# A two-block network in one program: five PSUM banks for dense products, zeros multiplied first, more context products behind the norms

## The chip, the cores and the metric

One Trainium2 chip, one core. The metric is the device time of one launch in microseconds, the median of repeated runs. Everything is computed in fp32 or in pairs of fp32r values (a rounded high part and the rest).

## What is computed

The reference chains two transformer blocks on a sequence of 256 tokens with a model width of 1024. The first block is a normalised mixer of three attentions with gates, then a convolutional feed-forward. The second block, run twice (layer 0 and layer 1), mixes a differential attention and a state-space scan (SSD) for two streams, the 256 latent tokens `x` and 256 context tokens `ctx`, each normalised and modulated by its own conditioning, and ends with a squared-ReLU MLP. Cut to what the change touches:

```
def modulate(x, g, shift, scale):
    return rmsnorm(x, g) * (1 + scale) + shift

for l in range(2):
    h_l = modulate(xl, norm_mix_g[l], mod_l[0], mod_l[1])
    h_c = modulate(xc, norm_mix_g[l], mod_c[0], mod_c[1])
    o_l, o_c = hybrid_mixer_2(h_l, h_c, ...)          # q, k, v, z, conv inputs, gates = h @ w_in
    xl = xl + mod_l[2] * o_l
    xl = xl + mod_l[5] * sq_relu_mlp(modulate(xl, norm_mlp_g[l], mod_l[3], mod_l[4]), w_mlp1[l], w_mlp2[l])
    ...                                               # the same for xc in layer 0
```

## The kernel before, in words

Activations lie transposed, features on the 128 partitions, eight tiles of 128 features each; `h` is such a set of eight (high, low) pairs, with columns 0 to 255 for the latent tokens and 256 to 511 for the context. A weight piece is 128 x 1024 values: SyncE loads it (`wr`), ScalarE rounds it (`wh`, L207), VectorE subtracts to get the rest (`wl`, L208). A dense product with one piece is 24 matmuls: for each of eight k-tiles high by high, high by low and low by high (L225 to L227 with the weight held in the array, L246 to L248 with the activation held).

The order on TensorE is written out: each stage is a Python generator of dense work (one or two steps for each product), and `weave` (L185) lets every generator in a list `bg` of background work go one step after each step of dense work. On the other engines the order comes from priorities. A background generator's `yield` therefore says how many dense steps lie between two of its pieces on TensorE. `wait` in `norm` (L284) adds such steps.

A norm (L284) squares the eight tiles on ScalarE (L296), adds them on VectorE (L298), sums over partitions with small matmuls (L307), takes the power on GpSimd (L269), makes diagonals on VectorE (L273, `dg`) and spreads them with a matmul (L281). `mod_norm` (L926) then makes for each tile `u` on VectorE (L939), `v` from it on GpSimd (L940), the high part on ScalarE (L941) and the low part on VectorE (L942). `u` and `v` come from `tmp()`; in the second block these are the pool `mt` with six buffers.

The places that the change touches, in order of time:

- the start of `first_block`: the products `prods_c` run on unnormalised activations while `pre_norm` computes the norm;
- the post-norm of the first block (`add_normed`, L871), behind which four products of the context's gates are woven (`gate_blocks`, pieces 72 to 75);
- the chain behind the feed-forward: `add_normed`, two empty steps, `mod_norm` for the second block (L859 to L863), behind which `ssd_lead` (L1078) computes `S.nv` value products of the context ahead of time, two dense steps each, stores them in `vd`, and `diff_front` (L1301) later loads them and leaves out the context half of that head pair's value product;
- in `layer`, the dense products behind the attention's last head pair: `diff_front` of head pair 3 and `gate_blocks` with pieces 80 to 87 (512 columns each in layer 0, in two steps);
- in `layer` 0, `mod_norm` of the MLP, woven into the first MLP products (`up`, L1628), whose results wait in PSUM for `r` (L1635) on ScalarE.

PSUM has eight banks: three for `mm` (dense products), three for `sm`, two for `lg` (used only by the SSD and by the attention).

Of the kernel before, what the change touches and what calls it, by code (L numbers as in the profile page):

```python
# [10 lines left out]
F32 = mybir.dt.float32  # L11
# [6 lines left out]
P = 128  # L18
# [80 lines left out]
class Net:  # L99
    def __init__(self, ctx, tc, A, stop=None, x_only=False):  # L100
# [11 lines left out]
        self.ps_lg = p("pslg", 2, space=PSUM)  # L112
        self.sp = p("sp", 2)
        self.HP = 100
        self.MW = 2
# [12 lines left out]
        nc = self.nc  # L128
# [5 lines left out]
        warm = self.cp.tile([P, 4], F32, name="warm")  # L134
        nc.scalar.activation(warm, self.nhalf, AF.Copy)

    def constants(self, first):
# [28 lines left out]

    def mm_ps(self, shape=(P, 512)):
        return self.ps_mm.tile(list(shape), F32, tag="mm", name="mm")

# [166 lines left out]
    def first_block(self, es_x):  # L336
# [5 lines left out]
        with ExitStack() as es:  # L342
# [46 lines left out]
            bc = []  # L389
# [3 lines left out]
            def pre_norm():  # L393
                t1 = lambda: p4.tile([P, 256], F32, tag="t1", name="hv")
                sq = []
                for c in range(4):
                    t = pb.tile([P, 2, 256], F32, tag=f"gate{c}", name="sq")
                    sq += [t[:, 0, :], t[:, 1, :]]
                yield from self.norm(x, lambda: sq.pop(), bc, start=True)
                nc.scalar.activation(rt, bc[0], AF.Copy)  # L400
                nc.vector.tensor_copy(rc, bc[1][:, 0:2])
                yield
                for k in range(8):
                    v = t1()
                    nc.vector.scalar_tensor_tensor(v, x[k], self.sm("pre_g", k), rt, op0=ALU.mult, op1=ALU.mult)
                    self.split(h[k][0], h[k][1], v)
# [343 lines left out]
            hcd = tc.dram_tile([8, P, 2, 256], F32, name="hcd")  # L750
            gd = self.gd = tc.dram_tile([8, P, 512], F32, name="gd0")

            def context():
# [14 lines left out]
            with self.in_order():  # L768
# [14 lines left out]

                bg = [self.add_normed(x, hs, "post_g", t16)]
                self.step(bg)
                self.weave(self.gate_blocks(W2[72:76], hc, 0, 256, spill(t1)), bg)
                while bg:
# [10 lines left out]
        with ExitStack() as es:  # L798
# [44 lines left out]
            with self.in_order():  # L843
# [15 lines left out]
                def chain():  # L859
                    yield from self.add_normed(x, [hs[k // 2][:, k % 2, :] for k in range(8)], "ffn_post_g", tmp, self.XP)  # L860
                    yield
                    yield
                    yield from self.mod_norm(0, 0, 0, x, h2, 0, tmp)  # L863

# [5 lines left out]

    def add_normed(self, x, hs, g, tmp, shared=()):  # L871

        nc = self.nc
        bc = []
        yield from self.norm(hs, tmp, bc)
        with self.tc.high_priority(offset=self.HP):
            for k in range(8):
                v = tmp()
                nc.vector.scalar_tensor_tensor(v, hs[k], self.sm(g, k), bc[0], op0=ALU.mult, op1=ALU.mult)
                (nc.gpsimd if k in shared else nc.vector).tensor_tensor(x[k], x[k], v, op=ALU.add)  # L880
# [44 lines left out]

    def mod_norm(self, l, i, s, x, h, t0, tmp, eng=None, wait=0, keep=None):  # L926

# [6 lines left out]
        with self.tc.high_priority(offset=(0,100)[i] if s == 0 else (0,0)[i]):  # L934
            for k in range(8):
                hi, lo = h[k][0][:, t0:t0 + 256], h[k][1][:, t0:t0 + 256]
                g, b = self.gsc[l][:, i, k, s:s + 1], self.mods[l][:, 24 * i + k, s:s + 1]
                u, v = tmp(), tmp()
                nc.vector.tensor_tensor(u, x[k], bc[0], op=ALU.mult)  # L939
# [109 lines left out]
    def ssd_open(self, l, h):  # L1049
# [22 lines left out]
        S.dT = S.p2.tile([64, 512], F32, tag="s2", name="dT")  # L1072
        S.nv = (3,2)[l]
        S.vd = self.tc.dram_tile([S.nv, P, 512], F32, name=f"vd{l}")
# [379 lines left out]
    def layer(self, l, x, S):  # L1454
# [5 lines left out]
        W = A["w_in_2"][l]  # L1460
        h = S.h
        yd = tc.dram_tile([16, P, T], F32, name=f"yd{l}")
        ad = tc.dram_tile([8, P, T], F32, name=f"ad{l}")
# [4 lines left out]
        def pool(es, name, bufs, sd):  # L1468
            return self.side_pool(es, f"{name}{l}", bufs, sd)
# [35 lines left out]
        with ExitStack() as es:  # L1505
# [25 lines left out]

            self.weave(self.gate_blocks(W[80:88], h, 0, T, keep), bg)
            while bg:
                self.step(bg)
        pt = pool(es_m, "mt", 6, "left")
        px = pool(es_x, "xc", 1, "left")
        streams = [(0, x, 0)]
# [15 lines left out]
        with self.in_order():  # L1553
# [48 lines left out]
            h = self.pairs(self.hp, 8, 512, "h")  # L1602
            tmp = lambda: pt.tile([P, 256], F32, tag="mt", name="nt")
            bg = []
            if last:
# [7 lines left out]
            for st in reversed(streams):  # L1613
                self.weave(self.residual(l, 2, [st], mg, A["w_out_2"][l]), bg)
                bg.append(self.mod_norm(l, 1, st[0], st[1], h, st[2], tmp, wait=0 if st[0] or last else self.MW,
                                        keep=rt if last else None))
        if not last:
            es_g.close()
        es_p.close()
        with ExitStack() as es, self.in_order():  # L1620
# [80 lines left out]
            for st in reversed(streams):  # L1701
                self.weave(self.residual(l, 5, [st], mid, A["w_mlp2_2"][l][24:]), bg)
                if not last:
                    if st[0] == 1:
                        h = self.pairs(self.hp, 8, 512, "h")
                        bg.append(self.mod_norm(1, 0, 1, xc, h, 256, tmp))
                    else:
                        S = self.ssd_open(1, h)
                        while bg:
                            self.step(bg)  # L1710
                        bg.append(self.mod_norm(1, 0, 0, x, h, 0, tmp))
                        self.weave(self.ssd_lead(S, 1), bg)
# [146 lines left out]
```

## Time and profile before

| what | value |
|---|---|
| median of 3 runs | 2579.7 us (2575.28 to 2581.87) |
| the profiled execution's own time | 2582.36 us |
| its span, first to last instruction | 2580.6 us |
| mean granted clock of TensorE | 0.991 |
| busy: TensorE, VectorE, ScalarE, GpSimd | 2507.5, 1900.0, 1423.5, 600.0 us |
| weight pieces split | 578 |

The profiled execution's own time is 1.8 us over its span and 2.7 us over the median of the runs. Busy shares are of the span. A granted clock of 1.00 is 2.4 GHz, one of 0.50 is 1.2 GHz.

### The profile page before, as it was taken

How to read it: one execution, taken by the hardware profiler on the slowest of the kernel's cores; microseconds unless marked ns; L12 is line 12 of the kernel's file. 1: busy time of each engine (PE TensorE's matmuls, PEld its weight loads, DVE VectorE, ACT ScalarE, POOL GpSimd, SP SyncE). 2: the span in 40 equal slices, each digit the busy share in tenths (PEclk: the TensorE clock that was granted, in tenths of full speed). 3: DMA queues.
4: the chain of work that ended last, by engine and by line, in shares of the span. 5: the costliest groups of instructions: out<-in, count | busy, mean ns of one | idle time of the engine just before them, and what ended most of it. 6: DMA issues, size and time to landing. Idle time of an engine off the chain costs nothing.

```text
span 2580.6 us, 44520 instructions
## 1 busy us (share of the span) xinstructions
PE 2507.5 (97%) x16698; PEld 2264.1 (88%) x16698; DVE 1900.0 (74%) x3102; ACT 1423.5 (55%) x2722; POOL 600.0 (23%) x645
## 2 busy tenths in 40 slices
PE   7999999999999999999999899999999999999998
PEld 7889999998888888878889888889788888899998
DVE  7887777877677775777796887647677767777665
ACT  5655665554656565676434633335565546665654
POOL 1001310111455564210022100003264432200000
PEclk9999999999999999999999999999999999999999
DMA  8666755663433444332674666525443353365552
GB/s 281 198 221 215 237 198 186 236 207 126 133 121 125 131 129 165 105 94 75 225 264 139 205 214 233 189 98 164 137 140 130 115 170 127 94 201 196 173 187 99
DMA packets 179766, 431.27 MB, mean 167 GB/s; under 512 B 18884, under 2 KB 84610, under 8 KB 179294
## 3 DMA queue, kind: packets, MB, share of 16 engines
q1 hardware_dynamic: 176254, 424.26, 49.1%
q0 software_dynamic: 2720, 3.64, 0.5%
q8 instruction: 132, 2.16, 0.3%
q14 instruction: 84, 0.69, 0.1%
q10 hardware_dynamic: 576, 0.52, 0.1%
HBM read 406.82 MB, written 18.32 MB: 165 GB/s over the span
## 4 chain that ended last, share of the span: by engine, by line
PE 73%; issue 10%; DVE 6%; ACT 5%; POOL 3%; DMA 3%; SPq 1%; POOLq 0%; DVEq 0%; ACTq 0%
PE mm L225 19%; PE mm L226 19%; PE mm L227 19%; PE mm L246 2%; PE mm L247 2%; PE mm L248 2%; PE sm L1258 1%; PE sm L1182 1%; ACT wh L207 1%; DVE wl L208 1%; DMA ru<-qk 1%; PE sm L1245 1%; SPq L1312 1%; PE lg L1401 1%; POOL nt L940 1%
## 5 line engine op out<-in xcount | busy, mean ns | idle before, releaser
L207 ACT ACTIVATE wh<-wr 128x1024 fp32r<-128x1024 f32 x578 | 610.2, 1057 | 636.3 <-PE mm L226 493.2
L208 DVE TENSOR_TENSOR wl<-wr,wh 128x1024 fp32r<-128x1024 f32 x578 | 733.2, 1271 | 281.4 <-ACT wh L207 268.8
L225 PE MATMUL mm<-h,wh 128*128 128x256 f32 (+1 forms) x2232 | 765.0, 343 | 12.3 <-ACT r L1635 7.0
L226 PE MATMUL mm<-h,wh 128*128 128x256 f32 (+1 forms) x2232 | 743.8, 333 | 4.0 <-DVE h L707 2.1
L227 PE MATMUL mm<-h,wl 128*128 128x256 f32 (+1 forms) x2232 | 744.7, 334 | 0.0
L225 PEld LDWEIGHTS mm<-h,wh 128*128 128x128 f32 x2232 | 422.1, 189 | 62.5 <-issue 7.3
L226 PEld LDWEIGHTS mm<-h,wh 128*128 128x128 f32 x2232 | 422.4, 189 | 54.0 <-issue 5.7
L227 PEld LDWEIGHTS mm<-h,wl 128*128 128x128 f32 x2232 | 421.4, 189 | 42.6
L225 PE MATMUL mm<-mid,wh 128*128 128x256 f32 (+1 forms) x832 | 254.9, 306 | 0.3 <-ACT mid L251 0.3
L227 PE MATMUL mm<-mid,wl 128*128 128x256 f32 (+1 forms) x832 | 254.1, 305 | 0.0
L226 PE MATMUL mm<-mid,wh 128*128 128x256 f32 (+1 forms) x832 | 253.6, 305 | 0.4 <-DVE mid L252 0.3
L246 PE MATMUL mm<-wh,h 128*128 128x256 f32 (+1 forms) x704 | 203.6, 289 | 1.2 <-ACT bc L1038 1.0
L247 PE MATMUL mm<-wl,h 128*128 128x256 f32 (+1 forms) x704 | 198.4, 282 | 0.0
L248 PE MATMUL mm<-wh,h 128*128 128x256 f32 (+1 forms) x704 | 198.3, 282 | 0.0
L225 PE MATMUL mm<-o,wh 128*128 128x256 f32 x592 | 167.3, 283 | 7.9 <-ACT wh L207 7.9
L227 PE MATMUL mm<-o,wl 128*128 128x256 f32 x592 | 167.2, 282 | 1.3 <-DVE wl L208 1.3
L226 PE MATMUL mm<-o,wh 128*128 128x256 f32 x592 | 167.1, 282 | 0.2 <-DVE o L252 0.2
L226 PEld LDWEIGHTS mm<-mid,wh 128*128 128x128 f32 x832 | 156.1, 188 | 9.0 <-DVE mid L252 1.0
L227 PEld LDWEIGHTS mm<-mid,wl 128*128 128x128 f32 x832 | 156.2, 188 | 8.4
L225 PEld LDWEIGHTS mm<-mid,wh 128*128 128x128 f32 x832 | 156.2, 188 | 7.6 <-ACT mid L251 0.5
L246 PEld LDWEIGHTS mm<-wh,h 128*128 128x128 f32 x704 | 135.1, 192 | 3.6 <-ACT bc L1038 1.2
L247 PEld LDWEIGHTS mm<-wl,h 128*128 128x128 f32 x704 | 135.2, 192 | 0.6
(371 smaller groups left out, 4737.3 us busy)
## 6 DMA issues: line engine op xcount, KB each, us to landing
wr<-in_w_in_dram SPq DMA_DIRECT2D x247, 512.0 KB, 3.7
wr<-in_w_mlp_dram SPq DMA_DIRECT2D x144, 512.0 KB, 4.3
wa<-in_adaT_dram SPq DMA_DIRECT2D x96, 512.0 KB, 4.4
wr<-in_w_up_dram SPq DMA_DIRECT2D x64, 512.0 KB, 4.4
wr<-in_w_out_dram SPq DMA_DIRECT2D x32, 512.0 KB, 3.5
wr<-in_w_down_dram SPq DMA_DIRECT2D x32, 512.0 KB, 4.4
wr<-in_w_ssd_o_dram SPq DMA_DIRECT2D x32, 512.0 KB, 4.3
E<-csd SPq DMA_DIRECT2D x24, 512.0 KB, 4.3
```

What stands on the lines that cost most here:

```text
L207: nc.scalar.activation(hi, raw, AF.Copy)
L208: nc.vector.tensor_tensor(lo, raw, hi.bitcast(F32), op=ALU.subtract)
L225: nc.tensor.matmul(ps, wh, xh, start=start and k == 0, stop=False)
L226: nc.tensor.matmul(ps, wh, xl, start=False, stop=False)
L227: nc.tensor.matmul(ps, wl, xh, start=False, stop=stop and k == n - 1)
L246: nc.tensor.matmul(ps, xh, wh, start=k == 0, stop=False)
L247: nc.tensor.matmul(ps, xh, wl, start=False, stop=False)
L248: nc.tensor.matmul(ps, xl, wh, start=False, stop=k == n - 1)
L940: nc.gpsimd.tensor_scalar(v, u, g, b, op0=ALU.mult, op1=ALU.add)
L1182: nc.tensor.matmul(ps[:, d0:d1, :], BN[:, c, :], xw[:, d0:d1].rearrange("p d h e -> p d (h e)"), start=True, stop=True)
L1245: nc.tensor.matmul(ps[:, d0:d0 + n].rearrange("p d h e -> p d (h e)"), C[:, ck * P:(ck + 1) * P], H[ck][:, d0:d0 + n, :], start=True, stop ...
L1258: nc.tensor.matmul(py[:, c, hh * 64:(hh + 1) * 64], E[sg][:, hh, c * P:(c + 1) * P], xN[:, 2 * sg + c, hh * 64:(hh + 1) * 64], start=True, ...
```

## The change

Seven edits. (1) `mm_ps` takes two of every five PSUM tiles from the `lg` pool, so that dense products go round five banks, except between the start of `layer` and the end of its attention. (2) Nine fp32 matmuls on a tile of zeros stand first on TensorE. (3) The norms at the start and behind the first mixer wait one dense step more. (4) Two context gate products (pieces 80 and 81) move from layer 0's attention to the post-norm, with results parked in `gc` in DRAM; layer 0 then computes these two for 256 columns only. (5) In the chain behind the feed-forward the two empty steps before `mod_norm` go, and its norm waits two steps more before its sums. (6) `S.nv` goes from (3, 2) to (4, 3): one more context value product ahead of each layer's SSD. (7) In layer 0 and at layer 1's start `u` and `v` of `mod_norm` are the halves of one `mt` tile.

```diff
@@ Net.__init__ and what it issues first
+        self.five, self.turn = True, 0
...
+        none = self.wl.tile([P, 8, P], F32, tag="wl", name="none")[:, :2, :].rearrange("p a b -> p (a b)")
+        nc.vector.memset(none, 0.0)
+        with self.in_order():
+            ps = self.sm_ps()
+            for _ in range(9):
+                nc.tensor.matmul(ps[:, :256], none[:, :P], none, start=True, stop=True)
@@ mm_ps
+        if self.five:
+            self.turn = (self.turn + 1) % 5
+            if self.turn % 2:
+                return self.lg_ps(shape)
         return self.ps_mm.tile(list(shape), F32, tag="mm", name="mm")
@@ pre_norm
-                yield from self.norm(x, lambda: sq.pop(), bc, start=True)
+                yield from self.norm(x, lambda: sq.pop(), bc, start=True, wait=1)
@@ first_block, behind the mixer
+            gc = self.gc = tc.dram_tile([2, P, 256], F32, name="gc0")
...
-                bg = [self.add_normed(x, hs, "post_g", t16)]
+                def early(i, make):
+                    t = t1()
+                    make(t)
+                    nc.sync.dma_start(gc[i], t)
+
+                bg = [self.add_normed(x, hs, "post_g", t16, wait=1)]
                 self.step(bg)
+                self.weave(self.gate_blocks(W2[80:82], hc, 0, 256, early), bg)
                 self.weave(self.gate_blocks(W2[72:76], hc, 0, 256, spill(t1)), bg)
@@ chain behind the feed-forward
-                    yield
-                    yield
-                    yield from self.mod_norm(0, 0, 0, x, h2, 0, tmp)
+                    yield from self.mod_norm(0, 0, 0, x, h2, 0, tmp, wait=2)
@@ mod_norm
-                u, v = tmp(), tmp()
+                u, v = two() if two else (tmp(), tmp())
@@ ssd_open
-        S.nv = (3,2)[l]
+        S.nv = (4,3)[l]
@@ layer: self.five = False at its start, True behind the attention
-            self.weave(self.gate_blocks(W[80:88], h, 0, T, keep), bg)
+            def halved(i, make):
+
+                gs.append(pg.tile([P, T], F32, tag="g", name="g"))
+                nc.sync.dma_start(gs[i][:, 256:], self.gc[i])
+                make(gs[i][:, :256])
+
+            n = 0 if last else 2
+            self.weave(self.gate_blocks(W[80:80 + n], h, 0, 256, halved), bg)
+            self.weave(self.gate_blocks(W[80 + n:88], h, 0, T, lambda i, make: keep(n + i, make)), bg)
...
+            def two():
+                t = pt.tile([P, 2, 256], F32, tag="mt", name="nt")
+                return t[:, 0, :], t[:, 1, :]
...
-                                        keep=rt if last else None))
+                                        keep=rt if last else None, two=None if last else two))
```

The two `mod_norm` calls of layer 0's end, which make layer 1's `h`, take `two=two` as well. The change adds 33 lines, so its own line numbers are higher.

**TensorE, the chain behind the feed-forward.** The sums of the second norm are the products of `cst` and `t`, the spread is the product `sm<-dg,cst`, and `mm<-h,wh 128x512` is the first product that needs the new `h`. Before, from the last sums on:

```order
L307 MATMUL sm<-cst,t_7584 128x1
L307 MATMUL sm<-cst,t_7595 128x1
L281 MATMUL sm<-dg,cst 128x128 x2
L225 MATMUL mm<-h,wh 128x512
L226 MATMUL mm<-h,wh 128x512
L227 MATMUL mm<-h,wl 128x512
```

Now, from the same sums on (L259 to L261 are the lines that were L246 to L248):

```order
L320 MATMUL sm<-cst,t_7604 128x1
L320 MATMUL sm<-cst,t_7615 128x1
L259 MATMUL mm<-wh,h 128x256
L260 MATMUL mm<-wl,h 128x256
L261 MATMUL mm<-wh,h 128x256
```

Between the sums and the spread there are now 24 products of the fourth context value piece, and 24 more between the spread and the first product with 512 columns; before there were none in either place.

**VectorE, `mod_norm` of layer 0's MLP for the latent tokens.** `nt<-xl` makes `u`, `h<-nt` the low half, `wl` is a weight piece. Before:

```order
L939 TENSOR_TENSOR nt<-xl_2748,sm 128x256
L942 TENSOR_TENSOR h<-nt,h 128x256
L939 TENSOR_TENSOR nt<-xl_2750,sm 128x256
L208 TENSOR_TENSOR wl<-wr,wh 128x1024
L942 TENSOR_TENSOR h<-nt,h 128x256 x2
L939 TENSOR_TENSOR nt<-xl_2752,sm 128x256
L208 TENSOR_TENSOR wl<-wr,wh 128x1024
L942 TENSOR_TENSOR h<-nt,h 128x256
L939 TENSOR_TENSOR nt<-xl_2754,sm 128x256
L208 TENSOR_TENSOR wl<-wr,wh 128x1024
L942 TENSOR_TENSOR h<-nt,h 128x256
L939 TENSOR_TENSOR nt<-xl_2756,sm 128x256
```

Now:

```order
L957 TENSOR_TENSOR nt<-xl_2763,sm 128x256
L960 TENSOR_TENSOR h<-nt,h 128x256
L957 TENSOR_TENSOR nt<-xl_2765,sm 128x256
L960 TENSOR_TENSOR h<-nt,h 128x256 x2
L957 TENSOR_TENSOR nt<-xl_2767,sm 128x256
L957 TENSOR_TENSOR nt<-xl_2769,sm 128x256
L957 TENSOR_TENSOR nt<-xl_2771,sm 128x256
L960 TENSOR_TENSOR h<-nt,h 128x256 x2
L957 TENSOR_TENSOR nt<-xl_2773,sm 128x256
L960 TENSOR_TENSOR h<-nt,h 128x256 x2
```

The four weight pieces that stood between the tiles of the norm now stand behind them.

**ScalarE, the same place.** `h<-nt` is the high half, `wh` a weight piece, `r` the evacuation of the MLP products' PSUM. Before:

```order
L941 ACTIVATE h<-nt,mod_86,gsc_88 128x256 x2
L207 ACTIVATE wh<-wr 128x1024
L941 ACTIVATE h<-nt,mod_86,gsc_88 128x256 x2
L207 ACTIVATE wh<-wr 128x1024
L941 ACTIVATE h<-nt,mod_86,gsc_88 128x256 x2
L207 ACTIVATE wh<-wr 128x1024
L941 ACTIVATE h<-nt,mod_86,gsc_88 128x256 x2
L1635 ACTIVATE r<-mm 128x256 x2
```

Now:

```order
L959 ACTIVATE h<-nt,mod_101,gsc_103 128x256 x3
L220 ACTIVATE wh<-wr 128x1024
L959 ACTIVATE h<-nt,mod_101,gsc_103 128x256 x5
L1668 ACTIVATE r<-lg 128x256
L1668 ACTIVATE r<-mm 128x256
```

The evacuations `r` stand behind the last high half in both, and two of the three weight pieces between the halves have moved behind them.

## Rows read from the trace of the kernel before

**Rows 1.** The page: the span, and TensorE's busy time.

```profile
span 2580.6 us, 44520 instructions
...
PE 2507.5 (97%) x16698; PEld 2264.1 (88%) x16698; DVE 1900.0 (74%) x3102; ACT 1423.5 (55%) x2722; POOL 600.0 (23%) x645
```

**Rows 2.** Waits of TensorE, whole span: total us, times, longest us.

```profile
PE sm L1377 <- ACT e L1381: 8.1, 10, 2.0
...
PE mm L225 <- ACT r L1635: 7.0, 1, 7.0
...
PE sm L510 <- ACT pt L630: 3.5, 1, 3.5
```

**Rows 3.** Stretches: length, TensorE's busy time (instructions), granted clock, DMA share, GB/s.

```profile
8.00:13.70 5.70, 4.80 (x21) 1.00 0.94 348
20.50:23.90 3.40, 3.40 (x18) 0.50 0.99 394
604.20:611.00 6.80, 4.57 (x12) 0.50 0.57 188
...
1454.40:1457.50 3.10, 3.07 (x14) 0.50 0.20 70
...
1050.00:1180.00 130.00, 123.95 (x740) 1.00 0.28 88
...
2150.00:2245.00 95.00, 89.22 (x592) 1.00 0.35 110
...
315.00:600.00 285.00, 284.84 (x2435) 1.00 0.61 209
```

**Rows 4.** Timeline of the start: from, us, engine, line, work [idle before].

```profile
9.50 3.88 DVE L387 SCALAR_TENSOR_TENSOR o<-xl,smt,o 128x256 fp32r<-128x256 f32 x6
...
14.90 0.39 PE L227 MATMUL mm<-o,wl 128*128 128x256 f32 x1 [0.35 <-DVE wl L208]
...
18.85 0.83 PE L307 MATMUL sm<-cst,sq 128*128 128x1 f32 x6 [0.99 <-DVE sq L298]
...
32.16 1.09 DVE L252 TENSOR_TENSOR h<-hv,h 128x256 fp32r<-128x256 f32 x3
...
37.04 0.70 PE L608 MATMUL sm<-sl,sl 64*128 64x256 f32 x2
```

**Rows 5.** Waits of TensorE, 255 to 320 us and 1800 to 1812 us.

```profile
PE sm L307 <- DVE t L298: 1.3, 1, 1.3
...
PE mm L226 <- DVE h L942: 1.1, 1, 1.1
PE mm L225 <- ACT h L941: 0.5, 2, 0.2
```

**Rows 6.** Timeline behind the feed-forward.

```profile
605.28 1.19 PE L281 MATMUL sm<-dg,cst 128*128 128x128 f32 x4 [2.48 <-DVE dg L273]
...
607.62 0.79 PE L225 MATMUL mm<-h,wh 128*128 128x512 f32 x1 [1.15 <-ACT h L941]
...
609.44 4.29 POOL L940 TENSOR_SCALAR t<-t,gsc,mod 128x256 f32<-128x256 f32 x5 [0.15 <-DVE t L939]
...
613.76 0.43 DVE L942 TENSOR_TENSOR h<-t,h 128x256 fp32r<-128x256 f32 x1 [0.46 <-POOL t L940]
```

**Rows 7.** Timeline of `mod_norm` in layer 0's MLP.

```profile
1441.53 4.09 POOL L940 TENSOR_SCALAR nt<-nt,gsc,mod 128x256 f32<-128x256 f32 x4 [4.94 <-DVE nt L939]
...
1448.96 1.37 POOL L940 TENSOR_SCALAR nt<-nt,gsc,mod 128x256 f32<-128x256 f32 x1 [0.99 <-DVE nt L939]
...
1454.02 0.64 ACT L1635 ACTIVATE r<-mm 128x256 f32<-128x256 f32 x2
```

**Rows 8.** Timeline of the attention's end, layer 0 and layer 1.

```profile
1237.10 0.69 DVE L1412 TENSOR_TENSOR sq<-lg,rr 128x512 f32<-128x512 f32 x1 [1.19 <-POOL rr L1411]
...
2294.33 0.41 PE L1419 MATMUL sm<-cst,sq 128*128 128x128 f32 x2 [1.27 <-DVE sq L1412]
```

**Rows 9.** The page: groups of instructions, the weight pieces on VectorE (busy, mean ns).

```profile
L208 DVE TENSOR_TENSOR wl<-wr,wh 128x1024 fp32r<-128x1024 f32 x578 | 733.2, 1271 | 281.4 <-ACT wh L207 268.8
```

More of the change, by code (lines that the diff above doesn't have):

```diff
@@ L869, in first_block, with add_normed @@
         return x, S
-    def add_normed(self, x, hs, g, tmp, shared=()):
+    def add_normed(self, x, hs, g, tmp, shared=(), wait=0):
         nc = self.nc
         bc = []
-        yield from self.norm(hs, tmp, bc)
+        yield from self.norm(hs, tmp, bc, wait=wait)
         with self.tc.high_priority(offset=self.HP):
@@ L924, in ada_finish, with mod_norm @@
                                                    self.sm(f"{('mix_g', 'mlp_g')[i]}{l}"), op0=ALU.add, op1=ALU.mult)
-    def mod_norm(self, l, i, s, x, h, t0, tmp, eng=None, wait=0, keep=None):
+    def mod_norm(self, l, i, s, x, h, t0, tmp, eng=None, wait=0, keep=None, two=None):
         nc = self.nc
@@ L1461, in layer @@
         h = S.h
+        self.five = False
         yd = tc.dram_tile([16, P, T], F32, name=f"yd{l}")
@@ L1535, in layer @@
         pt = pool(es_m, "mt", 6, "left")
+        self.five = True
         px = pool(es_x, "xc", 1, "left")
@@ L1705, in layer @@
                         h = self.pairs(self.hp, 8, 512, "h")
-                        bg.append(self.mod_norm(1, 0, 1, xc, h, 256, tmp))
+                        bg.append(self.mod_norm(1, 0, 1, xc, h, 256, tmp, two=two))
                     else:
@@ L1710, in layer @@
                             self.step(bg)
-                        bg.append(self.mod_norm(1, 0, 0, x, h, 0, tmp))
+                        bg.append(self.mod_norm(1, 0, 0, x, h, 0, tmp, two=two))
                         self.weave(self.ssd_lead(S, 1), bg)
```

## The prediction

> **What bounds the kernel now.** The page comes first. TensorE is busy for 2507.5 of 2580.6 us [rows 1], so at most 73 us are waits, and an edit on another engine is worth only what it takes from these. The list of TensorE's waits comes next: a single wait of 7.0 us for a PSUM evacuation, ten waits of 8.1 us together in the attention, one of 3.5 us at the start [rows 2]. The list of stretches is third, for what the list of waits cannot show: behind a wait the granted clock falls to 0.50, and a product takes twice its time [rows 3]. In the long stretch from 315 to 600 us, 2435 products take 285 us, 0.117 us each, with next to no waiting [rows 3]; there the change can gain nothing, and a dense step of 24 products is 24 x 0.117 = 2.8 us of cover wherever it is put. So I look place by place at who ends the wait, and then at what the moved work leaves behind.
>
> **Behind the feed-forward (edits 5 and 6).** TensorE waits 2.48 us for the spread's diagonals and 1.15 us for the first high half [rows 6]. The clock then stands at 0.50 for 6.8 us, in which TensorE is busy 4.57 [rows 3]; at full clock that is half, so 2.3 us are lost. Together 5.9 us. Now a dense step of 2.8 us lies between sums and spread, more than the 2.48, and another between spread and the first product that needs `h`, more than the 1.15. What is late next is the last tiles of `h`: GpSimd takes 4.29 / 5 = 0.86 us for each `v` [rows 6]. The sums end at 605.28 - 2.48 = 602.8; a step and the spread later it is 606, and the eighth low half comes near 606 + 8 x 0.86 + 0.43 = 613.3, and two weight pieces of 1.27 us [rows 9] now stand among the tiles on VectorE, so 613.3 to 615. TensorE, which before was slowed by the clock and got the last low half at 613.76 [rows 6], now starts a step later, at 609, and takes 6 x 0.117 = 0.70 us a tile, so it wants the eighth at about 614. I take 0.6 us of new waiting (bounds 0 and 1.5). Net **-5.3**.
>
> **The MLP of layer 0 (edits 1 and 7).** TensorE stands for 7.0 us because `r` has not emptied a bank [rows 2]; `r` ran at 1454.02 [rows 7], behind all eight high halves in ScalarE's order. The first four tiles took GpSimd 1.02 us each, the later ones 1.37 with 0.99 of idling before each [rows 7]: `u` waited for one of six buffers, which hold three tiles of `u` and `v`, and weight pieces stood between the tiles on VectorE. Behind the stop 3.07 us of products ran at clock 0.50 [rows 3], another 1.5 us. With both halves in one buffer the pool holds six tiles and VectorE's order is free of weight pieces. GpSimd then sets the pace, between 0.86 us a tile [rows 6] and 1.37, where VectorE ran weight pieces beside it [rows 7]. At 1.0 us, the nearest to the first four, eight tiles from 1441.5 end at 1449.5, so `r` follows near 1449 and not at 1454. With five banks TensorE does not stop at 1447.4 (1454.4 less 7.0) but begins the first product that reads the new `h`; it wants the eighth tile at 1447.4 + 7 x 0.35 = 1450, and the next weight piece, now queued behind the norm on VectorE, at 1450.7. Both are near misses: I take 1.0 us (bounds 0.3 and 4). Net 7.0 + 1.5 - 1.0 = **-7.5**.
>
> **Post-norm and layer 1's start (edits 3, 4, 6).** The sums wait 1.3 us for VectorE; at 1806 the products of the new `h` wait 1.1 + 0.5 us [rows 5]. Two dense steps more stand before each. Net **-1.3** and **-1.6**; a piece of either could stay, hardly more could come.
>
> **The start (edits 2 and 3).** TensorE waits 0.99 us for the adds [rows 4], and the clock dips to 0.50 for 3.4 us [rows 3], 1.7 us lost. The first 21 products take 4.80 us, 0.23 each [rows 3], the lower level, although the column reads 1.00. Yet VectorE sets the time here: it makes the low halves of the raw activations without a break from 9.50 to 13.38 [rows 4], the second product waits for the `wl` of its piece until 14.90 [rows 4], and the normalised `h` ends at 33.2 on VectorE [rows 4], whose order holds the same work now, some of it ahead of the last `h`. A TensorE that arrives earlier waits there. I take **-0.5**, bounds +2.8 and -2.7. The zeros are covered: nine fp32 products at up to 0.70 us [rows 4] and twice that at the lower clock are 6 to 13 us, and the first real product of 2.8 us cannot end before its last low half at 13.4; at the upper end 2.8 us of it could stick out, which is the bound above zero.
>
> The Trainium skill's page "TensorE: Matmul & The Clock Gate" (section Part 1: The HAM clock gate) says that the throttled clock is the default and that activity releases it. By that rule the zeros would release the clock before the first real product, and the start would give 21 x (0.23 - 0.117) = 2.4 us more if TensorE set the time there.
>
> **What pays for it.** The moved products were cover in the attention. Layer 0 loses four dense steps behind its third head pair (two of the value product, two of the gates), layer 1 two. Between 1050 and 1180 TensorE loses 130 - 123.95 = 6.0 us over three head pairs, between 2150 and 2245 95 - 89.22 = 5.8 over about three [rows 3]: 2 us where a pair has the shorter front. Layer 0's last pair now looks like these: +1.0 (bounds 0 and 2). Layer 1's third likewise: +0.5 (bounds 0 and 2). In layer 0 the last pair needs 15 steps and the gates now give 14, so the last transposes stand uncovered: they wait for `sq`, which VectorE ends at 1237.8 [rows 8], about when the last dense step would end; layer 1 ends so already and waits 1.27 us [rows 8]. +0.5 (bounds 0.3 and 1.3). Sum **+2.0**, bounds 0.3 and 5.3.
>
> **Counted at nothing.** Six more weight pieces (584 for 578) of 1.27 us on VectorE [rows 9]: two each at the three places that get two dense steps, one piece a step of 2.8 us; uncovered, 1.3 us each. Two products of 512 columns become four of 256; the columns are the same. Parking gates in `gc` and values in `vd` costs SyncE one store and one load each; the loads stand in its queue behind stores of the SSD or behind head pair fronts, where their buffers have long been free, so no weight piece waits behind them. Banks from `lg`: nothing else uses them where `five` is on.
>
> **Sum.** -5.3 - 7.5 - 1.3 - 1.6 - 0.5 + 2.0 = -14.2. The profiled execution took 2582.4 us, so 2568.2; it lay 2.7 over the median of the runs, which gives **2565.5 us**.
>
> **The rivals.**
> *The norm in the MLP stays late.* If GpSimd needs 1.37 us a tile [rows 7], the eighth low half comes at 1441.5 + 11 + 0.4 = 1453, 3 us late, and the weight piece behind it follows. For it: that pace was measured in this very stretch. Against: it stood beside weight pieces, which are gone from there. New waits 4 us, not 1: 2568.5. Chance 0.12.
> *The start is worth its full price.* If TensorE's lead carries to the wait of 3.5 us [rows 2] and removes it with 1.7 for a dip like that of [rows 3], and the 0.99 and 1.7 of the sums and the 2.4 of the first products come too, it is 10 us and not 0.5; a half of it is what could be kept: 2561. For it: all these waits are in the rows. Against: VectorE without a break. By the page's rule alone it would be 2563. Chance 0.12.
> *The cover was worth more than the norms give (slower).* The six steps moved out of the attention are 6 x 2.8 = 16.7 us. If none of them is used there to wait for anything else, TensorE stands for all of it, in the tails of head pairs 2 and 3, with two dips of 1.7: the attention costs 20, not 2, and the sum is +3.9: 2583.6. It decides against the change from 16 us lost on. Against it: in layer 0 the same fronts, two steps shorter, lose only 2 us a pair. Chance 0.05 for that; 0.10 for a loss of 8 to 9 us in which SSD and attention fall into a worse rhythm: 2572 to 2575.
> *The buffers do nothing.* If ScalarE's queue and not the buffers held `r`, five banks alone give 5.6 us of the 7.0 and the dip returns: 2568 to 2570, inside the first rival's range. Chance 0.05.
>
> **How the numbers follow.** The forecast holds 0.56. Its own bounds, 2561 to 2571, come from the terms' bounds, of which not all fall on one side. The range that leaves out 2 in 10 reaches into the start's full price and into the worse rhythm: **2555 to 2577**. No change means within 0.3%, 7.7 us, of 2579.7, about what a measurement can tell: under 2572.0 is faster. The forecast, the first two rivals and the last lie there nearly whole, 0.79 of 0.85; the worse rhythm, the edge of the others and most of the lost cover lie within, 0.18; over 2587.4 remains 0.03.
>
> **What would show it.** Right: no wait over 0.5 us at the spread behind the feed-forward, and no stretch of 0.50 there; no wait of TensorE for `r` L1635 (now L1668), with the eight `u` issued in under 8 us; no wait at layer 1's first products; waits for `e` in the attention's last head pair of layer 0, about 1 us, and one for the last `sq`; at the start products 0.117 us apart from the first, but the same wait for the second `wl` and the attention's first wait of about 3.5 us still there. Wrong: a wait of several us at the MLP's first product on the new `h`; a start that ends 5 us earlier; or attention stretches that lose more than 8 us in either layer.

## The result and the profile after

The changed kernel takes 2555.6 us (median of 4 runs, 2552.3 to 2561.9) against 2580.8 for the kernel before, timed beside it: a ratio of 0.9897, 95% interval 0.9876 to 0.9917, so 25 us less by the medians and 26.6 by the ratio. Timed twice more on other chips it gave 0.9898 and 0.9881. The forecast of -14.2 us has the direction and about half of the size. 2555.6 lies just inside its range of 2555 to 2577, but before was 1 us slower in this comparison than in the one that the forecast started from: the ratio applied to that 2579.7 gives 2553.1, and the two other timings give 2553.4 and 2549.0, all below the range. The profiled execution of the changed kernel is the slowest of its four: 2561.9 us, 20.4 under the profiled one of before.

The page of the changed kernel, span and TensorE:

```profile
span 2560.1 us, 44683 instructions
...
PE 2509.2 (98%) x16764; PEld 2266.5 (89%) x16764; DVE 1904.8 (74%) x3109; ACT 1427.3 (56%) x2730; POOL 594.0 (23%) x645
```

TensorE's waits fall from 73 us [rows 1] to 51. Of these 22 us, 7 are no gain: the zeros now fill the wait for the first weight piece, 7.9 us before, which leaves 1.2 ahead of the zeros themselves. The list of TensorE's waits, whole span (total us, times, longest us):

```profile
PE sm L1395 <- ACT e L1399: 5.6, 6, 2.5
...
PE lg L1419 <- ACT at L1412: 3.5, 6, 1.3
...
PE sm L1437 <- DVE sq L1430: 2.7, 1, 2.7
...
PE sm L294 <- DVE dg L286: 2.1, 3, 1.4
...
PE sm L143 <- DVE none L139: 1.2, 1, 1.2
PE sm L523 <- ACT pt L558: 1.2, 1, 1.2
```

and two more of the list of before:

```profile
PE mm L225 <- ACT wh L207: 7.9, 1, 7.9
...
PE lg L1401 <- ACT at L1394: 2.3, 4, 0.8
```

The 7.0 us for `r` and the 3.5 us for `pt` L630 [rows 2] are gone, the waits for `e` in the attention fell from 8.1 to 5.6 while those for `at` rose from 2.3 to 3.5, and 2.7 us for the last `sq` is new in size: layer 1 waited 1.3 there [rows 8]. The wait for `pt` L558 is at another product, at 165 us.

**Behind the feed-forward**, waits of TensorE from 588 to 625 us:

```profile
PE mm L239 <- DVE h L960: 1.1, 1, 1.1
PE sm L320 <- DVE t L311: 0.9, 1, 0.9
PE mm L238 <- ACT h L959: 0.5, 2, 0.2
```

The spread no longer waits (before 2.48 us, [rows 6]) and no stretch there stands at 0.50, but the new `h` is awaited for 1.6 us in three places, where before it was 1.15 in one.

**The MLP of layer 0**, timeline of GpSimd (from, us, engine, line, work):

```profile
1431.54 2.94 POOL L958 TENSOR_SCALAR nt<-nt,gsc,mod 128x256 f32<-128x256 f32 x4 [4.93 <-DVE nt L957]
1434.64 3.37 POOL L958 TENSOR_SCALAR nt<-nt,gsc,mod 128x256 f32<-128x256 f32 x4 [0.16 <-DVE nt L957]
```

and of ScalarE:

```profile
1433.81 2.96 ACT L959 ACTIVATE h<-nt,mod,gsc 128x256 fp32r<-128x256 f32 x5
1436.67 0.36 ACT L1668 ACTIVATE r<-lg 128x256 f32<-128x256 f32 x1
```

Eight tiles take GpSimd 6.5 us, 0.81 each, instead of 1.02 to 1.37 with idling between [rows 7], and `r` follows the last high half at once.

**Stage by stage.** I cut four executions at the same events, the first of each norm's sums (L307), the first products of SSD (L1013 in layer 0, L1191 in layer 1) and attention, and the last sums of layer 1's attention (L1419), read off their timelines. Lengths in us; "null" is the kernel before with one idle addition (below), "whole" the change on the same chip as null. "Moved" is the work that the change carries in or out: a dense step is 24 products at 0.117, 2.8 us.

| stage | before | after | null | whole | moved | net, after - before | net, whole - null | forecast |
|---|---|---|---|---|---|---|---|---|
| start, first attention | 266.9 | 267.7 | 268.2 | 268.5 | 0 | +0.8 | +0.3 | -0.5 |
| post-norm | 36.0 | 40.2 | 36.0 | 40.5 | +5.6 | -1.4 | -1.1 | -1.3 |
| feed-forward | 285.3 | 281.8 | 283.1 | 281.8 | 0 | -3.5 | -1.3 | 0 |
| chain | 52.1 | 54.6 | 52.6 | 54.7 | +5.6 | -3.1 | -3.5 | -5.3 |
| SSD, layer 0 | 406.9 | 405.1 | 407.9 | 403.1 | 0 | -1.8 | -4.8 | 0 |
| attention, layer 0 | 358.4 | 346.2 | 359.3 | 346.2 | -11.2 | -1.0 | -1.9 | +1.5 |
| MLP, layer 0 | 366.1 | 357.5 | 370.0 | 357.5 | 0 | -8.6 | -12.5 | -7.5 |
| layer 1's start | 74.2 | 78.2 | 75.8 | 78.4 | +5.6 | -1.6 | -3.0 | -1.6 |
| SSD, layer 1 | 304.6 | 301.0 | 301.8 | 301.0 | 0 | -3.6 | -0.8 | 0 |
| attention, layer 1 | 144.1 | 142.0 | 146.4 | 142.7 | -5.6 | +3.5 | +1.9 | +0.5 |
| to the end | 286.1 | 285.9 | 285.9 | 287.8 | 0 | -0.2 | +1.9 | 0 |
| sum | 2580.6 | 2560.1 | 2586.9 | 2562.3 | 0 | -20.5 | -24.6 | -14.2 |

Two things stand out: the MLP, larger than forecast, and the stages with the same products before and after (feed-forward, SSD; only the feed-forward's PSUM banks differ), which are 9 us shorter in one pair and 7 in the other. Null does the work of before in the same order on every engine, and still the two differ by 2.2 us in the feed-forward, 2.8 in layer 1's SSD and 3.8 in the MLP, so a single pair of traces can be off by as much. The last column's term for the post-norm holds, that for layer 1's start in the first pair.

### The profile page after: what moved, and what is told of

Its sections match the earlier page's. It is cut to its first block, busy times and chain, and to the rows that moved or that the text cites. A ratio compares the mean times of both kernels' runs of the same rounds, so it can differ in the third digit from the quotient of the medians.

```text
span 2560.1 us, 44683 instructions
## 1 busy us (share of the span) xinstructions
PE 2509.2 (98%) x16764; PEld 2266.5 (89%) x16764; DVE 1904.8 (74%) x3109; ACT 1427.3 (56%) x2730; POOL 594.0 (23%) x645
## 4 chain that ended last, share of the span: by engine, by line
PE 75%; issue 9%; DVE 6%; ACT 4%; POOL 3%; DMA 2%; SPq 1%; POOLq 0%; DVEq 0%; ACTq 0%
PE mm L238 14%; PE mm L239 14%; PE mm L240 14%; PE lg L238 6%; PE lg L240 6%; PE lg L239 6%; PE mm L259 2%; PE mm L260 2%; PE mm L261 2%; PE sm L1200 1%; PE sm L1276 1%; PE sm L1263 1%; ACT wh L220 1%; DMA ru<-qk 1%; DVE wl L221 1%
## 5 line engine op out<-in xcount | busy, mean ns | idle before, releaser
L238 PE MATMUL mm<-h,wh 128*128 128x256 f32 (+1 forms) x1736 | 607.3, 350 | 4.4 <-DVE cv L1062 3.3
L239 PE MATMUL mm<-h,wh 128*128 128x256 f32 (+1 forms) x1736 | 588.7, 339 | 2.5 <-DVE h L960 1.7
L240 PE MATMUL mm<-h,wl 128*128 128x256 f32 (+1 forms) x1736 | 589.1, 339 | 0.0
L238 PEld LDWEIGHTS mm<-h,wh 128*128 128x128 f32 x1736 | 329.2, 190 | 46.5 <-issue 5.7
L239 PEld LDWEIGHTS mm<-h,wh 128*128 128x128 f32 x1736 | 329.5, 190 | 45.4 <-issue 5.7
L259 PE MATMUL mm<-wh,h 128*128 128x256 f32 (+1 forms) x672 | 194.9, 290 | 0.3 <-ACT wh L220 0.3
L261 PE MATMUL mm<-wh,h 128*128 128x256 f32 (+1 forms) x672 | 190.3, 283 | 0.0
L239 PE MATMUL lg<-h,wh 128*128 128x256 f32 (+1 forms) x496 | 154.2, 311 | 2.3 <-DVE h L720 2.1
L238 PE MATMUL lg<-h,wh 128*128 128x256 f32 (+1 forms) x496 | 156.1, 315 | 0.3 <-ACT h L719 0.3
L240 PE MATMUL lg<-h,wl 128*128 128x256 f32 (+1 forms) x496 | 154.6, 312 | 0.0
L238 PE MATMUL mm<-mid,wh 128*128 128x256 f32 (+1 forms) x492 | 150.4, 306 | 0.3 <-ACT mid L264 0.3
L239 PE MATMUL mm<-mid,wh 128*128 128x256 f32 (+1 forms) x492 | 149.7, 304 | 0.4 <-DVE mid L265 0.3
L240 PE MATMUL mm<-mid,wl 128*128 128x256 f32 (+1 forms) x492 | 150.0, 305 | 0.0
L259 PEld LDWEIGHTS mm<-wh,h 128*128 128x128 f32 x672 | 130.1, 194 | 2.3 <-issue 0.9
L261 PEld LDWEIGHTS mm<-wh,h 128*128 128x128 f32 x672 | 129.9, 193 | 0.0
L926 DVE SCALAR_TENSOR_TENSOR th<-wa,cb 128x1024 bf16<-128x1024 f32 x96 | 121.9, 1277 | 10.4 <-DMA wa<-in_adaT_dram 9.8
L1062 DVE SCALAR_TENSOR_TENSOR cv<-mm,cwh,cv 128x510 f32<-128x510 f32 (+1 forms) x128 | 94.1, 740 | 16.3 <-ACT cv L1056 14.8
```

The source lines that it names most:

```text
L238: nc.tensor.matmul(ps, wh, xh, start=start and k == 0, stop=False)
L239: nc.tensor.matmul(ps, wh, xl, start=False, stop=False)
L240: nc.tensor.matmul(ps, wl, xh, start=False, stop=stop and k == n - 1)
L259: nc.tensor.matmul(ps, xh, wh, start=k == 0, stop=False)
L261: nc.tensor.matmul(ps, xl, wh, start=False, stop=k == n - 1)
L926: nc.vector.scalar_tensor_tensor(junk, raw, 0.5, self.cb[:, s, :], op0=ALU.mult, op1=ALU.mult, accum_out=self.mods[l][:, 2 * i + m, s:s + 1])
```

## The experiments

All medians are from five rounds; "before" is timed beside each, on the same chip: 2585.1 us for the first four kernels, 2590.6 for the next four, 2592.7 and 2591.6 for the last two fours. So only ratios compare across groups.

| kernel | median us | against before | ratio, 95% interval |
|---|---|---|---|
| start's edits alone | 2580.4 | -4.7 | 0.9984 (0.9976 to 0.9993) |
| post-norm's alone | 2580.0 | -5.2 | 0.9979 (0.9968 to 0.9990) |
| chain and value products alone | 2578.9 | -6.2 | 0.9970 (0.9958 to 0.9983) |
| five banks and one tile alone | 2563.1 | -22.0 | 0.9918 (0.9905 to 0.9931) |
| whole change | 2564.5 | -26.1 | 0.9898 (0.9882 to 0.9915) |
| five banks alone | 2577.5 | -13.1 | 0.9946 (0.9930 to 0.9962) |
| one tile alone | 2580.9 | -9.7 | 0.9958 (0.9944 to 0.9972) |
| whole without five banks | 2565.8 | -24.8 | 0.9907 (0.9890 to 0.9923) |
| null | 2590.9 | -1.9 | 0.9994 (0.9979 to 1.0008) |
| whole without one tile | 2571.4 | -21.4 | 0.9915 (0.9892 to 0.9939) |
| whole without chain and values | 2565.7 | -27.1 | 0.9897 (0.9875 to 0.9918) |
| whole without start's edits | 2560.8 | -31.9 | 0.9874 (0.9852 to 0.9896) |
| whole, third time | 2562.2 | -29.4 | 0.9881 (0.9864 to 0.9898) |
| whole without start's edits, again | 2558.8 | -32.8 | 0.9870 (0.9854 to 0.9885) |
| and layer 1's third value product out | 2559.2 | -32.4 | 0.9876 (0.9863 to 0.9889) |
| whole without the zeros alone | 2559.4 | -32.2 | 0.9876 (0.9863 to 0.9889) |

**One part each on the kernel before.** Each kernel is the one before with some lines of the change's diff: the start's with (2) and the first norm's `wait=1`; the post-norm's with (4) and its own `wait=1`; the chain's with (5) and (6); the MLP's with (1) and (7). Of each the core (cut):

```diff
@@ the start's
+            for _ in range(9):
+                nc.tensor.matmul(ps[:, :256], none[:, :P], none, start=True, stop=True)
@@ the post-norm's
+                self.weave(self.gate_blocks(W2[80:82], hc, 0, 256, early), bg)
@@ the chain's
+        S.nv = (4,3)[l]
@@ the MLP's
+        self.five, self.turn = True, 0
+                u, v = two() if two else (tmp(), tmp())
```

> The kernel before with two edits alone: the zeros multiplied first, and one more dense step ahead of the sums of the first norm. My forecast's term for the start says -0.5 us against before (2580.3 if before repeats its 2580.8), with the wait of 3.5 us at the attention's first product still there. The rival that the start is worth its full price says -5 to -10 (2571 to 2576). A third theory, that a good part of the 25 us lies in stretches of clock 0.50 whose number changes from kernel to kernel, says -0.5 within 3, with a time that follows the mean granted clock of each run.

> The kernel before with the post-norm's edits alone: one more dense step ahead of its sums, and two gate products of the context moved there out of layer 0's attention. My terms: -1.3 for the wait that goes, +0.5 for the cover that the last head pair loses (bounds 0 and 2): -0.8 us, about 2580. The theory that the attention loses nothing for it says -1.3 or lower; that the cover was worth more says +1 or higher.

> The kernel before with the chain behind the feed-forward alone: the two empty steps gone, two steps more ahead of the second norm's sums, and one context value product more ahead of each layer's SSD. My terms: -5.3 (chain), -1.6 (layer 1's start), +1.5 (cover lost in the attention): -5.4 us, about 2575.4. The theory that the attention pays nothing and may run better says -7 to -10, with no more waiting in the stretch of layer 0's attention than the 7.9 us of before. The trace of the whole change shows its chain 3.7 us shorter and not 5.3.

> The kernel before with five PSUM banks and with both halves of a norm's temporaries in one tile, and nothing else. My term: -7.5 us, about 2573.3, with no wait for r. In the trace of the whole change the stretch from the MLP's norm to layer 1's start is 8.6 us shorter, so the theory that the terms are right and add up says -7.5 to -9; the theory that five banks help elsewhere too says -10 or lower, with shorter stretches outside the MLP.

The three small parts measure some 5 us each, the MLP's 22: three times its term. Added up they are 38 us, and the whole change gives 25 to 29, so they overlap. Nor do they all lie where the edits are: with the start's edits alone the first stage is 268.3 us, against 266.9 before. With the MLP's alone its own stage is 357.5 us, as in the whole change, 8.6 us under before and 12.5 under null, so 10 us or more of the 22 lie elsewhere. But the stage differs between kernels that leave it alone. The stretch of the MLP with the start's edits alone (stretch, its length, then busy time and instructions of TensorE, weight loads, VectorE, ScalarE, GpSimd, then clock, DMA share, GB/s):

```profile
1402.27:1773.58 371.31, 360.28 (x1942) 310.66 (x1941) 253.47 (x413) 156.83 (x233) 29.19 (x25) 0.99 0.54 182
```

and TensorE's longest waits in it:

```profile
PE mm L238 <- ACT r L1668: 7.0, 1, 7.0
PE mm L238 <- DVE xc L1766: 3.4, 4, 1.9
```

The second wait is TensorE at a bank that the residual's additions on VectorE (L1733 of the kernel before) have not emptied. The profiled execution of before has none of it (nor has that of the chain's edits alone, 367.9 us), and its 366.1 us are the shortest of five executions with three banks and two buffers (366.1, 367.9, 370.0, 371.2, 371.3).

**The MLP's two edits apart, and the whole without the banks.** One tile alone is the kernel with the MLP's edits and the first lines below undone, five banks alone the same kernel with the last lines undone; the whole change without five banks has the first lines undone.

```diff
-        self.five, self.turn = True, 0
+        self.five, self.turn = False, 0
@@ behind the attention
-        self.five = True
+        self.five = False
@@ or instead, at the MLP's call of mod_norm (at layer 1's two calls `two=two` goes)
-                                        keep=rt if last else None, two=None if last else two))
+                                        keep=rt if last else None, two=None))
```

> The whole change again, timed together with its pieces. Taken apart, the MLP's edits gave -22 us and not the -7.5 of my term, the start, the post-norm and the chain each -5 to -6. If the parts added up in full it would be -38 us against before; the first comparison gave -25. I expect -26 to -32, so the parts overlap: each of them takes away some of the same waits.

> The kernel before with five banks for dense products alone, the temporaries of the norms in two buffers as before. My fourth rival puts it at 5.6 of the 7.0 us, the stop for r shrunk to 1.4 us: -6, and nothing anywhere else. The theory that three banks stop TensorE in many places that the one profiled execution of before did not show (other executions show waits for the VectorE additions of the residuals, 3.4 and 0.9 us) says -12 or lower, with these waits gone.

> The kernel before with both halves of a norm's temporaries in one tile alone, three banks as before. By my working r follows near 1449 and not 1454, so the stop of 7.0 us shrinks to about 2, and its slow stretch may go: -5 to -6.5, and at layer 1's start another 1 us or so. The theory that the banks are what counts says the same -5 to -6.5 here and leaves the rest to the banks; the theory that the buffers do everything says -18 or lower.

> The whole change without five banks: every dense product in three banks again. If my terms were right this loses some 5 us against the whole change (the stop for r returns in part). If the banks carry half of the gain, it loses 12 us or more, so -14 to -18 against before.

Waits in the MLP's stage with five banks alone:

```profile
PE lg L232 <- DVE h L954: 2.8, 3, 1.0
PE lg L231 <- ACT h L953: 1.2, 3, 0.5
```

and with one tile alone:

```profile
PE mm L231 <- DVE xc L1759: 3.8, 5, 1.8
PE mm L231 <- DVE xl L1759: 0.4, 1, 0.4
```

With five banks TensorE passes the stop for `r` and then waits six times for the slow norm, with 6.8 us at clock 0.50: 365.7 us. With one tile the stop is gone too, wholly and not to 2 us, but the residuals still find three banks too few: 364.1. Against 369.3, the mean of the five traces above, that is 3.6 and 5.2 us; together they give 11.8, and next to nothing is left to wait for. Of the 11.8, 8.2 us are waits (TensorE is idle for 8.8 us in the mean of the five, for 0.6 with both) and 3.6 are the same products in less time:

```profile
1400.55:1758.07 357.52, 356.92 (x1942) 309.16 (x1941) 252.74 (x413) 156.12 (x233) 24.60 (x25) 1.00 0.57 189
```

That is the stretch of the kernel with both. My fourth rival had it right that five banks alone pass the stop and that the slow stretch returns, but not its 5.6 us: the waits for the slow norm take 4.0 of them back. The Trainium skill's page "Perfetto Trace Analysis" (section Matmul Optimizations) says to use all eight PSUM banks; here five alone gain 3.6 of the 11.8 us, as long as the norm is slow. Medians do not follow the stages, though: five banks alone gave -13, and taking them out of the whole cost only 1.3. In the profiled execution without them the MLP is 363.7 us, 6.2 over the whole change's, with 4.2 us of waits for the residuals' additions, but its stretch from 2400 to 2540 us ran 5 us faster than the whole's (last section).

**Null, and the whole change less one part.** Null is the kernel before with this added to a line of its start; no other instruction changes or moves:

```diff
+        pad = self.cp.tile([P, 64], F32, name="pad"); nc.gpsimd.memset(pad, 0.0)
```

The other three are the whole change with these lines undone:

```diff
@@ without one tile
-                                        keep=rt if last else None, two=None if last else two))
+                                        keep=rt if last else None, two=None))
@@ without the chain and the values
-                    yield from self.mod_norm(0, 0, 0, x, h2, 0, tmp, wait=2)
+                    yield
+                    yield
+                    yield from self.mod_norm(0, 0, 0, x, h2, 0, tmp)
-        S.nv = (4,3)[l]
+        S.nv = (3,2)[l]
@@ without the start's edits
-            for _ in range(9):
-                nc.tensor.matmul(ps[:, :256], none[:, :P], none, start=True, stop=True)
-                yield from self.norm(x, lambda: sq.pop(), bc, start=True, wait=1)
+                yield from self.norm(x, lambda: sq.pop(), bc, start=True)
```

> The kernel before with one idle addition: GpSimd fills a 128 x 64 tile that nobody reads, and every instruction of the other engines stays as it was. If the -5 us that each of the small parts gave belongs to their own work, this one stands at 0 within 2 us. If before is unlucky in something that any edit disturbs (its products of 256 columns stand at the slower of two paces in the feed-forward, 117.05 ns against 115.3 in the changed kernel), this gives -3 to -5 us as well, and a feed-forward near 115.3 ns a product. In either case its trace is a second look at the waits of the kernel before.

> The whole change with the norms' temporaries in two buffers again. By my forecast this loses most of the MLP's 7.5 us. In the stretch of the MLP five banks alone gained 0.4 us, one tile alone 2.0, both 8.6, so there I expect +8 against the whole change, about -18 against before.

> The whole change without its edits to the chain behind the feed-forward and without the extra value products. My terms say +5.3 +1.6 -1.5 = +5.4 us against the whole change. In the trace the chain's stretch gained 6.6 us, of which 3.1 is the pace of products that the other parts bring too, layer 1's start 3.0 and the attention of layer 1 lost 3.5: so +3 to +5. If the parts overlap as the first comparison says (-38 in parts, -26 in one), 0 to +2.

> The whole change without the zeros and without the extra step ahead of the first norm's sums. My term says +0.5 us against the whole change; the rival of the start's full price says +5 to +10. In the trace of the whole change the stretch up to the post-norm is 0.8 us longer than before, with a stretch of 10 us at clock 0.50 in it that before does not have: so without these edits the time could even fall by 1 to 2 us.

Null is unchanged within its interval, but the interval reaches from -5.4 to +2.1 us, and its feed-forward is 283.1 us, not 285.3. So it does not show that the 5 us of each small part are the edits' own work, nor that they are a gain that any disturbance brings; that stays open. It waits for `r` and for the residuals alike:

```profile
PE mm L225 <- ACT r L1635: 7.0, 1, 7.0
PE mm L225 <- DVE xc L1733: 1.6, 3, 0.8
```

Without one tile the whole change loses 8 us (-21.4 against before; the whole, timed later on the same chip, -29.4), as expected. Without the chain it loses 2, not resolved by the intervals, where my terms add up to 5.4. Without the start's edits it is faster, if anything.

**The start once more, on one chip.** The second kernel undoes the same lines of the start as above. The third does too, and has

```diff
-        S.nv = (4,3)[l]
+        S.nv = (4,2)[l]
```

The fourth leaves out only the products of zeros, and keeps the `wait=1`.

> The whole change, on the chip of its three variants: -25 to -27 us against before, as in both comparisons so far, with 357.5 us for the stretch of layer 0's MLP and a stretch of 10 to 14 us at clock 0.50 from 38 us on.

> The whole change without the zeros and without the extra step ahead of the first norm's sums, a second time. If the start's edits cost (TensorE arrives earlier at the first products of the normalised h, waits there, and its clock falls to 0.50 for 10 us or more), this is 2 to 6 us faster than the whole change on the same chip. If they are worth what they gave alone, 4 us slower. My forecast's term says 0.5 us slower.

> The same as the run before and, in addition, two context value products ahead of layer 1's SSD as in the kernel before, not three. In the traces the third one gains 0.6 us at layer 1's start and loses 2.1 in its attention: so 1.5 us faster than without the start's edits alone, some 4 to 7 faster than the whole change. My forecast's terms (-0.6 for what is left of it at the start, +0.5 in the attention) say no difference.

> The whole change without the zeros alone; the extra step ahead of the first norm's sums stays. If the zeros are what makes TensorE early at the products of the normalised h, the time is that of the kernel without both; if the extra step is, that of the whole change.

TensorE's waits in the timeline of the whole change, third time, 30 to 60 us:

```profile
33.95 0.38 PE L239 MATMUL mm<-h,wh 128*128 128x256 f32 x1 [0.23 <-DVE h L265]
...
35.35 0.38 PE L238 MATMUL mm<-h,wh 128*128 128x256 f32 x1 [0.54 <-ACT h L264]
...
36.08 0.38 PE L239 MATMUL mm<-h,wh 128*128 128x256 f32 x1 [0.35 <-DVE h L265]
```

and the stretch behind them:

```profile
37.60:51.20 13.60, 13.60 (x65) 13.60 (x65) 11.79 (x18) 8.50 (x12) 0.77 (x1) 0.50 0.74 260
```

It is early, waits three times for the normalised `h`, and then runs 13.6 us at 0.50, 65 products at 0.21 us each, which costs half of that; in exchange the wait of 3.5 us for `pt` at 54.9 us is gone. Without the zeros the same three waits appear, so the extra step ahead of the sums brings them, but the slow stretch comes later and is 6.8 us, and `pt` is awaited for 4.0. Nor do zeros and step together always bring the early slow stretch: with the start's edits alone, and in the whole without one tile, it stands at 53 us, beside a wait of 4.0 for `pt`, and what decides that is open. The three variants lie 2.8 to 3.5 us under the whole change, all inside each other's intervals: in the whole change the edits at the start show no gain, though alone they measured -4.7; that the zeros cost is likely and not shown; and layer 1's third value product makes no difference. None of the three is shown to beat the changed kernel.

## Why the forecast was wrong in size

Two steps failed: the stages that I put at nothing gained 9 and 7 us, the largest miss in both pairs, and the MLP's term was too small by 1 and 5. The terms that missed the other way (chain, start, layer 1's attention) hide a part of this in the sum.

- **The MLP, -7.5: mis-sized.** The mechanism was right, the buffers made the norm quick and the new waits (1.0 assumed) are nil. Against the execution that I read it is -8.6, and what is missing there is that 1.0; against null it is -12.5. The term took the stops of a single execution as the kernel's. Three banks also stop at the residuals' additions, by 0.9 to 4.2 us in five of the other six traces with three banks, and the list of waits that I read did not have it.
- **"There the change can gain nothing": false.** The feed-forward has the same 2438 products and next to no waits, and still went from 285.3 to 281.8 us. I took the time of a product, 0.117 us, for fixed; it is 0.1156 now. What brings that is open (last section). Before:

```profile
302.87:588.16 285.29, 285.13 (x2438) 284.92 (x2437) 227.06 (x334) 168.63 (x257) 39.22 (x41) 1.00 0.64 215
```

and after:

```profile
307.88:589.66 281.78, 281.78 (x2438) 281.78 (x2437) 225.66 (x333) 168.86 (x257) 39.33 (x41) 1.00 0.64 219
```

- **The SSD, 0: gained 5.4 and 5.6 us over both layers**, although its work is the same. Some of it is time at 0.50 (three such stretches of 3.4 us in layer 1's SSD before, one after), some shorter waits (TensorE idle for 15.4 us over both layers before and 13.9 after; 18.7 in null and 14.6 in the whole). Which edit brings this is not settled; the post-norm's and the chain's parts alone show 402.3 and 401.3 us in layer 0 where null has 407.9.
- **The clock.** I counted 3.8 us for two dips. The granted clock, averaged over the runs, rose from 0.9899 (before) to 0.9927 (whole, third time): time at half clock falls by 2 x 0.0028 x 2575 = 14 us, so by this estimate 7 us of the 29 come from dips; in the profiled pair, 37.4 and 34.0 us at 0.50 ahead of the last microseconds, it is 1.7. It goes with this that the medians differ by 25 where the profiled executions differ by 20: of the changed kernel's four runs the fastest takes 2552.3 us at a granted clock of 0.995 and the slowest, the profiled one, 2561.9 at 0.992.
- **The chain, -5.3: -3.1 and -3.5.** The spread's wait and the slow stretch went as worked out; the late tiles of `h` cost 1.6 us, just past my upper bound of 1.5 and 1.0 over what I took, and the sums wait 0.9 as before. The other 0.8 to 1.2 us that are missing are not accounted for.
- **The cover, +2.0: +2.5 and 0.0 over both layers, but shared out otherwise.** Layer 0's attention lost nothing; its waits for `e` even fell. Layer 1's pays 3.5 in the first pair: its waits rise by 1.6 us (for `at` and for the last `sq` by 1.4 each, while those for `e` fall by 1.3), and 3.9 us stand at 0.50, where before had none. Over the nine traces with the third value product there, the price against before lies between -0.4 and 4.2 us.
- **Post-norm -1.3 and layer 1's start -1.6 held in the first pair** (-1.4 and -1.1; -1.6 and -3.0). But at layer 1's start the two steps more are not the only edit that takes the waits: TensorE is idle for 1.7 us there before, for 0.2 with the chain's edits alone, but also for 0.6 with the MLP's alone and for 0.95 with the one tile alone, which I had priced only in the MLP. The kernel with the MLP's edits alone has 71.8 us there against 74.2.
- **The start, -0.5: +0.8 and +0.3**, for the reason given: a TensorE that arrives earlier waits for VectorE. That its clock then falls for over 10 us was not in the sum, and the wait of 3.5 us that I named as a sign is gone, against the forecast. The rival of the start's full price is refuted: the stage does not get shorter. The Trainium skill's page "TensorE: Matmul & The Clock Gate" (section Part 1: The HAM clock gate) says that activity releases the throttled clock; the trace agrees, with products that come at twice the rate from 7.4 us on instead of 13.7, but the time does not follow.
- **The other rivals.** A norm that stays late: refuted by 0.81 us a tile. Cover worth more: no. Buffers that do nothing: refuted by one tile alone, without a wait for `r`.

## What to carry to other kernels

Before a term is put on a stop at a shared resource, look at several executions: one list of waits shows where this execution stopped, not where the kernel can stop. A stretch without waits is not yet one whose time is fixed. Two causes that guard the same stop, here the number of banks and the speed of what empties them, are priced together and not each alone. Work that makes an engine arrive earlier at a place where another one sets the time gained nothing here, and may cost its clock.

## What was not expected of the hardware

Products of 256 columns run at different paces with no wait and the clock at 1.00, and a pace can hold for tens of microseconds: 113.3 ns from start to start, 117.8, and in parts of the feed-forward a repeating pattern of 113 to 120 ns that averages 116.7. The stretch from 556 to 580 us, before:

```profile
556.00:580.00 24.00, 24.00 (x206) 24.00 (x205) 16.85 (x21) 10.95 (x16) 0.74 (x1) 1.00 0.59 197
```

and after:

```profile
556.00:580.00 24.00, 24.00 (x214) 24.00 (x213) 18.30 (x25) 13.79 (x21) 1.42 (x2) 1.00 0.64 212
```

The one has 206 products in the 24 us, the other 214 (those cut by an edge counted); from start to start they take 117.8 and 113.3 ns on average. From 2400 to 2540 us every kernel ran at the slower pace but the whole change without five banks, and the changed kernel for its last microseconds. The whole without five banks:

```profile
2400.00:2540.00 140.00, 139.93 (x1230) 139.70 (x1230) 92.43 (x126) 84.71 (x136) 0.00 (x0) 1.00 0.55 172
```

and the whole change, third time:

```profile
2400.00:2540.00 140.00, 139.92 (x1188) 139.72 (x1187) 89.80 (x121) 82.85 (x133) 0.00 (x0) 1.00 0.52 169
```

42 products more in the same time, 42 x 0.118 = 5 us. In the feed-forward the eleven traces with the post-norm's edits, one of them with these alone, all show 281.8 us and the other seven 282.2 to 285.3, null 283.1. The three traces of the changed kernel agree in both stretches (281.8 us; 1188 to 1191 products), so the pace seems to go with the program more than with the execution. What sets it was not found; nothing that I read in the profile differs between the two.
